# Retention keys and queries and attention keys of the latent rows by seven block products instead of eight, with the context products ahead of them and the modulation sums after them

## The chip, the cores and the metric

The kernel runs on one core of one Trainium2 chip. The metric is the device time of one execution in microseconds (us). TensorE multiplies matrices (operands in SBUF, results in PSUM); VectorE (DVE in the profile), ScalarE (ACT) and GpSimd (POOL) work elementwise; SyncE (SP) mostly issues DMAs. Each engine executes its own queue in order; semaphores order the engines among each other. The order within each queue is fixed when the kernel is built: a scheduler goes through the instructions by their order in the source, and takes a later one earlier when it is ready before the others.

## What is computed

One layer of a diffusion backbone: 1024 latent tokens and 256 context tokens, width 1024, float32. The part that matters here is the input projection, whose seven column blocks of 512 are retention queries (block 0), retention keys (1), retention values (2), gate (3), attention queries (4), attention keys (5) and attention values (6).

```python
m_lat = sc @ w_mod[l] + b_mod[l]
sh1, sc1, g1, sh2, sc2, g2 = ...
h_lat = rms_norm(x, norm1_g[l]) * (1.0 + sc1) + sh1
h_ctx = rms_norm(ctx, norm1_g[l]) * (1.0 + csc1) + csh1
(rq_l, rk_l, rv_l, rg_l), (dq_l, dk_l, dv_l) = split_heads(h_lat @ w_in, rope_r, rope_d)
(rq_c, rk_c, rv_c, rg_c), (dq_c, dk_c, dv_c) = split_heads(h_ctx @ w_in, None, None)
...
x = x + g1 * y_lat                                  # after retention, attention, output projection
h2 = rms_norm(x, norm2_g[l]) * (1.0 + sc2) + sh2    # then the gated MLP with a conv of width 3
x = x + g2 * conv_ffn(h2, ...)
```

Latent queries and keys are rotated by position (`apply_rope`), context keys are not. Of the context only keys and values are used.

## The kernel before

Every float32 operand of the large products is split into a high and a low half, and `passes` (L128) makes a product of three matmuls: high by high, high by low, low by high. A matmul takes 128 rows of the sum over the width (one k) and up to 512 columns; a full product over the width has 8 k, hence 24 matmuls.

- `hT[a][i]` (L174) are the normalized latent rows, transposed: a = 0 the high half, 1 the low half; i the half of the tokens; 8 k by 512 tokens each. `cT[a]` are the 256 context rows in the same form.
- Weights come in slices of two k: `slice_load` (L186) fetches 512 KB into a raw tile (`raw`, pool `wr`, 2 buffers) and `split_slice` (L195) makes `whi` on ScalarE and `wlo` on VectorE (pool `wp`, 5 buffers of each). `stream_block` issues the four slices of a block. From block 5 on the lists `raw_pools` and `slice_pools` add one more raw buffer and one more pair from the pool `m2p`; after block 0 they drop out again.
- `natural` computes 128 tokens by 512 columns (24 matmuls of 512 columns per tile), `transposed` computes one head (128 columns) by 512 tokens, also 24 matmuls. After each k both call `tick()`, which advances a generator that runs beside: it issues a bit of other work in between.
- `rotated` turns a result of `transposed` by position: ScalarE copies swapped 32- or 64-row parts out of PSUM, VectorE makes two products with the tables (`rtab`) and a sum. Attention keys are then split in two halves (`split_store`) and stored to HBM; retention keys and queries are stored as they are. For retention keys `natural_copy` turns the tile back on TensorE and scales it twice; for retention queries `decayed` multiplies it on GpSimd by `qd`, once for each direction.
- `modulations` computes the four late parts of the modulation (groups 0 to 3: g1, sh2, sc2, g2): 32 weight tiles of 512 KB, each multiplied into a sum by a VectorE operation of 128x1024 (L511), then a few matmuls with ones per group (`modulated2`). It runs beside blocks 5, 1 and 0, one step per 7 ticks.

The order of the stages: block 2 for latents, with the normalization; block 2 for the context; block 5 for latents, in its middle the context keys (`pc`, 256 columns); block 6 for the context; the small terms of decay and lambda (`lg`, `dec`, `qd`, `kd`, `cd`); block 1 for the context and for latents; block 0; then block 3 with the backward states of retention beside it, block 6 with the retention outputs beside it, block 4, attention, output projection (`po`), and the MLP. The MLP's first half already makes its products in the seven-product form (`chain`, `second`, `third`, `fifth` from L1300 on).

## Time and profile before

| what | value |
|---|---|
| time of three runs | 1386.96, 1388.20, 1388.31 us; median 1388.2 |
| span of the profiled execution | 1386.3 us (first to last instruction) |
| TensorE clock granted, mean | 0.999 |
| block 2, context (start to start) | 81.4 to 92.3 us |
| block 5 with context keys | 92.3 to 149.4 us |
| block 6 and block 1, context | 149.4 to 172.7 us |
| block 1, latents | 172.7 to about 221 us |
| block 0, latents | about 221 to 269.4 us |
| block 3, latents | 269.4 to 321.6 us |
| attention ends, output projection begins | about 645 us |
| output projection ends | about 744 us |

The page's lists name lines of the kernel; a line of a helper (L131 to L133 in `passes`) collects many uses, so the tile names beside it tell them apart: `pl` is `transposed`, `pn` is `natural`, `pc` the context keys, `chain`, `second`, `third`, `fifth` the MLP's products, `po` the output projection. The time of a run is a little over its span, since the span leaves out what lies before the first and after the last instruction.

### The profile page before, as it was taken

Reading aid. Unit: us, or ns where it says so; the run is one execution under the profiler, and the core shown is the slowest. Engines: PE = TensorE matmul, PEld = TensorE weight load, DVE = VectorE, ACT = ScalarE, POOL = GpSimd, SP = SyncE. Lnnn points to the kernel's source line nnn. Section 1 sums busy time; section 2 is a strip of 40 time slices with the busy share of each in tenths; the row PEclk is TensorE's granted clock in tenths of the full one; section 3 lists DMA queues with packets and bytes.
Section 4 is the critical chain, followed back from the end, with each engine's and each line's share of the span. In section 5 each row is a group of like instructions: output and inputs, shape, how many; then the busy total and the mean of one; then the engine's idle time right before and its main releaser. Section 6 shows DMA issues by size and latency. Waiting matters only on the chain.

```text
span 1386.3 us, 19666 instructions
## 1 busy us (share of the span) xinstructions
PE 1365.4 (98%) x7028; PEld 1145.9 (83%) x7028; DVE 1018.0 (73%) x1512; ACT 738.6 (53%) x1410; POOL 346.4 (25%) x384
## 2 busy tenths in 40 slices
PE   8999999999999999999999999999999999999997
PEld 6788788888888799998888888888888888888886
DVE  5967866623467898896347998887778877898756
ACT  5536534313466789987037654555545555455533
POOL 1310001501446433411101343222332220043003
PEclk9999999999999999999999999999999999999999
DMA  9467887786678488631221223332323326953334
GB/s 384 153 206 252 295 265 249 254 273 185 191 221 231 133 217 186 140 94 70 106 99 46 92 107 114 114 114 92 114 100 113 111 69 224 393 180 109 122 99 152
DMA packets 107305, 231.14 MB, mean 167 GB/s; under 512 B 9604, under 2 KB 42884, under 8 KB 105288
## 3 DMA queue, kind: packets, MB, share of 16 engines
q1 hardware_dynamic: 98936, 204.73, 43.3%
q0 software_dynamic: 8128, 24.91, 7.9%
q8 instruction: 55, 0.90, 0.3%
q14 instruction: 42, 0.34, 0.1%
q10 hardware_dynamic: 144, 0.26, 0.1%
HBM read 165.37 MB, written 64.23 MB: 166 GB/s over the span
## 4 chain that ended last, share of the span: by engine, by line
PE 65%; DVE 1%; POOL 1%; issue 0%; ACT 0%; DMA 0%; SPq 0%; POOLq 0%; ACTq 0%; DVEq 0%
PE chain L131 6%; PE chain L132 6%; PE chain L133 6%; PE c L132 5%; PE c L133 5%; PE c L131 5%; PE pv L929 5%; PE pA L897 5%; PE third L131 3%; PE third L133 3%; PE third L132 3%; PE pt L917 2%; PE po L133 2%; PE po L132 2%; PE po L131 2%; PE second L131 1%
## 5 line engine op out<-in xcount | busy, mean ns | idle before, releaser
L131 PE MATMUL pl<-hT,whi 128*128 128x512 f32 x256 | 107.6, 420 | 0.0
L131 PE MATMUL chain<-T,whi 128*128 128x512 f32 x264 | 102.8, 389 | 0.0
L132 PE MATMUL chain<-T,whi 128*128 128x512 f32 x264 | 102.7, 389 | 0.0
L133 PE MATMUL chain<-T,wlo 128*128 128x512 f32 x264 | 102.7, 389 | 0.0
L133 PE MATMUL pl<-hT,wlo 128*128 128x512 f32 x256 | 100.4, 392 | 0.0
L132 PE MATMUL pl<-hT,whi 128*128 128x512 f32 x256 | 100.3, 392 | 0.0
L900 DVE TENSOR_REDUCE mt<-pA 128x1 f32<-128x1280 f32 x64 | 95.2, 1490 | 3.8 <-PE pA L897 2.3
L133 PE MATMUL c<-whi,ghl 128*128 128x512 f32 x232 | 90.4, 390 | 0.0
L131 PE MATMUL c<-whi,ghl 128*128 128x512 f32 x232 | 90.3, 389 | 0.0
L132 PE MATMUL c<-wlo,ghl 128*128 128x512 f32 x232 | 90.3, 389 | 0.0
L1310 POOL TENSOR_TENSOR cmb<-wrb 128x512 f32<-128x512 f32 x20 | 30.3, 1517 | 237.6 <-DMA wrb<-w_up 157.3
L897 PE MATMUL pA<-ks,qhl 128*128 128x512 f32 (+1 forms) x384 | 89.6, 368 | 0.0
L904 ACT ACTIVATE p<-pA,mt 128x1280 f32<-128x1280 f32 x64 | 85.5, 1336 | 3.8 <-DVE mt L900 3.4
L131 PE MATMUL pn<-whi,hT 128*128 128x512 f32 x192 | 85.0, 443 | 0.0
L445 ACT ACTIVATE xb<-pl 32x512 f32<-32x512 f32 (+1 forms) x88 | 52.0, 591 | 61.6 <-PE pl L133 41.9
L1161 ACT CAST whi<-cmb 128x512 fp32r<-128x512 f32 x62 | 38.4, 622 | 77.5 <-PE chain L132 64.3
L929 PE MATMUL pv<-va,aT 128*128 128x128 f32 x640 | 77.1, 276 | 0.4 <-DVE yT L958 0.3
L897 PEld LDWEIGHTS pA<-ks,qhl 128*128 128x128 f32 x384 | 67.9, 189 | 11.5
L133 PE MATMUL pn<-whi,hT 128*128 128x512 f32 x192 | 75.8, 396 | 1.0 <-POOL hT L610 1.0
L132 PE MATMUL pn<-wlo,hT 128*128 128x512 f32 x192 | 75.4, 393 | 0.0
L929 PEld LDWEIGHTS pv<-va,aT 128*128 128x128 f32 x640 | 74.0, 192 | 1.2 <-DVE yT L958 0.8
L1162 DVE TENSOR_TENSOR wlo<-cmb,whi 128x512 fp32r<-128x512 f32 x62 | 58.7, 951 | 18.1 <-ACT whi L1161 18.1
(336 smaller groups left out, 3889.7 us busy)
## 6 DMA issues: line engine op xcount, KB each, us to landing
raw<-w_in SPq DMA_DIRECT2D x32, 512.0 KB, 6.0
wm<-w_mod SPq DMA_DIRECT2D x32, 512.0 KB, 4.6
wra<-w_up SPq DMA_DIRECT2D x24, 512.0 KB, 3.3
wrb<-w_up SPq DMA_DIRECT2D x23, 512.0 KB, 3.5
W<-w_down SPq DMA_DIRECT2D x44, 256.0 KB, 6.2
ad<-s SPq DMA_DIRECT2D x20, 512.0 KB, 3.4
wra<-ad SPq DMA_DIRECT2D x20, 512.0 KB, 3.3
wrb<-ad SPq DMA_DIRECT2D x18, 512.0 KB, 4.6
```

Source lines behind the costliest of these rows:

```text
L131: mm(ps, lh, rh, start=first, stop=False, skip_group_check=more)
L132: mm(ps, lh, rl, start=False, stop=False, skip_group_check=more)
L133: mm(ps, ll, rh, start=False, stop=last, skip_group_check=more)
L445: nc.scalar.activation(xb[q * blk : (q + 1) * blk, :], pt[o : o + blk, :], AF.Copy, scale=scale)
L897: mm(self.pa[m][:, c0:c1], self.q[:, i, m, qs], self.k[:, m, c0:c1], start=(i == 0), stop=(i == 1))
L900: nc.vector.tensor_reduce(out=self.mt[:, m : m + 1], in_=self.pa[m][:, :LK], axis=AX.X, op=ALU.min)
L904: nc.scalar.activation(self.p[m], self.pa[m][:, :LK], AF.Exp, scale=-1.0, bias=self.mt[:, m : m + 1], accum_out=self.s[:, m : m + 1])
L917: nc.tensor.transpose(self.pt[g][:, i, :], self.p[0][:, (4 * g + i) * P : (4 * g + i + 1) * P], ident)
L929: mm(self.pv, self.aT[:, c, :], self.v[:, c, :], start=(c == 0), stop=(c == NKT - 1))
L1161: nc.scalar.copy(hi, src)
L1162: nc.vector.tensor_tensor(out=lo, in0=src, in1=r32(hi), op=ALU.subtract)
L1310: nc.gpsimd.tensor_tensor(out=s1, in0=b1, in1=b2, op=ALU.add)
```

## The change

For blocks 5, 1 and 0 the latent rows (1024 wide, 1024 tokens) and the weights of two heads (1024 by 256) are cut in two by two blocks, and the four result blocks (two heads by two halves of tokens) are made from seven block products of half the width (4 k each) in place of eight. The sums and differences of weights (`combined`) are made on GpSimd, those of the rows (T1 to T4) on GpSimd and VectorE while the context products run. T1 takes the place of the first half of `hT[a][1]`, which is put aside in HBM (`h12_d`) and fetched back for block 3; T4 takes the place of `cT` once the context is done with. So the context products of blocks 2, 6, 1 and 5 come first, one after the other. Modulation groups 0 and 3 now run beside blocks 3 and 6, groups 1 and 2 beside the output projection. The weights come from a second copy in HBM (`w_pair`), two heads' worth per pair. The extra raw and slice buffers of `m2p` are gone. The swap of rotated parts becomes DMAs from SBUF to SBUF, except for one of the four results.

```diff
+PAIRED = (5, 1, 0)
...
-        raw_pools = [lambda: wr] * 2
-        slice_pools = [lambda: wp] * 5
...
+        for a in range(2):
+            nc.sync.dma_start(out=h12_d[a], in_=r32(hT[a][1][:, 0:4, :]))
...
+        B11, B21 = (tuple(hT[a][0][:, c : c + 4, :] for a in range(2)) for c in (0, 4))
+        T1, B22 = (tuple(hT[a][1][:, c : c + 4, :] for a in range(2)) for c in (0, 4))
+        T2, T3 = (tuple(tq.tile([P, 4, 512], F32R, name=f"tq{i}{a}") for a in range(2)) for i in (2, 3))
+        T4 = tuple(head_rows(t.rearrange("p k l -> p (k l)")) for t in cT)
...
+        def split_to(src, tt, c):
+            nc.scalar.copy(tt[0][:, c, :], src)
+            nc.vector.tensor_tensor(out=tt[1][:, c, :], in0=src, in1=r32(tt[0][:, c, :]), op=ALU.subtract)
+
+        def whole(name, hf, k, bufs=2):
+            o = tm.tile([P, 512], F32, name=name, bufs=bufs)
+            nc.gpsimd.tensor_tensor(out=o, in0=r32(hT[0][hf][:, k, :]), in1=r32(hT[1][hf][:, k, :]), op=ALU.add)
+            return o
...
+        def fourth_sums():
+            for c, t2 in enumerate(second):
+                t4 = whole("r12", 0, c + 4)
+                nc.gpsimd.tensor_tensor(out=t4, in0=t4, in1=t2, op=ALU.subtract)
+                split_to(t4, T4, c)
+
+        beside(block_sums(), 0.24, 0.0)
+        natural(wget, ctx_lhs, range(NTC), store_to(kvg_row(ROW_V), center=True))
+        wg = stream_block(6)
+        natural(wg, ctx_lhs, range(NTC), store_to(dv_row))
         wg = stream_block(1)
-        rtab = load_rope(0)
+        small_terms()
         natural(wg, ctx_lhs, range(NTC), context_decayed)
-        transposed(wg, [q[:, :, 1] for q in rqk_d], rtab, 64, RET_SCALE, 0, by_head, True)
-        wg = stream_block(0)
-        transposed(wg, [q[:, :, 0] for q in rqk_d], rtab, 64, 1.0, 0, by_head, also=decayed)
+        wg = stream_block(5)
...
+        beside(iter(()), 0.0)
+        fourth_sums()
...
+        er = erS.enter_context(tc.tile_pool(name="er", bufs=2, reuse_waits="tile"))
...
+        first_ops = [er.tile([P, 2, 4, P], F32R, name="xhl") for _ in range(2)]
...
+                self.ops = dict(p1=a1, p2=a2, p3=b1, p4=b2, p5=s1, p6=s2, p7=s3)
+                self.combos = ((s1, b1, b2, ALU.add), (s2, s1, a1, ALU.subtract), (s3, a1, b1, ALU.subtract), (b1, a2, s2, ALU.subtract))
...
+            def product(self, ps, p, tt, first):
+                o = self.halves.pop(p)
+                for k in range(4):
+                    passes(ps, (o[:, 0, k, :], o[:, 1, k, :]), (tt[0][:, k, :], tt[1][:, k, :]), first and k == 0, k == 3, not first)
+                    tick()
...
+            def turned(self, u, xb, c, hf):
+                cs, sn = self.rtab(hf)
+                (nc.vector if self.block == 0 else nc.gpsimd).tensor_tensor(out=xb, in0=xb, in1=sn, op=ALU.mult)
+                nc.vector.tensor_tensor(out=u, in0=u, in1=cs, op=ALU.mult)
+                nc.vector.tensor_tensor(out=u, in0=u, in1=xb, op=ALU.add)
+                self.kept(u, c, hf)
...
+            def begin(self):
+                self.chain = ps_a.tile([P, 512], F32, name="chain", tag="mm")
+                self.product(self.chain, "p1", B11, True)
+                second = ps_b.tile([P, 512], F32, name="second", tag="mm")
+                self.product(second, "p2", B21, True)
+                u = self.copied()
+                self.plus(u, second)
+                self.u11 = u, self.swapped(u)
...
+            def seventh(self):
+                self.product(self.chain, "p7", T3, False)
+                u = self.copied()
+                self.plus(u, self.other)
+                self.u22 = u, self.swapped(u)
+
+            def third(self):
+                self.product(self.other, "p3", B22, False)
+                self.plus(self.u12, self.other)
+                self.u12 = self.u12, self.swapped(self.u12)
...
+        for j in range(N_PAIRS):
+            one, more = prs[j], j + 1 < N_PAIRS
...
+            one.sixth()
...
+            one.fifth()
+            one.turned(*one.u11, 0, 0)
...
+            one.seventh()
...
+            if j > 0:
+                prs[j + 1].begin()
+            one.turned(*one.u22, 1, 1)
...
+            one.third()
...
+            one.fourth()
...
+        also(modulations((0, 3), ..., 6, ...), 1.0, 0.0)
...
+        beside(modulations((1, 2), norm_weights, norm_sums, 4, lambda: pst, None), 1.0)
```

The pairs go in the order two of block 5, then one of block 1, one of block 0, one of block 1, one of block 0. `begin` of pairs 0 and 1 comes ahead of the loop; from pair 2 on it stands between `seventh` and `third` of the pair before. `block_sums` makes T1, T2 and T3 chunk by chunk like `fourth_sums`. The last pair's `third` and `fourth` are issued inside the first tile of block 3.

More of the change, by code (lines that the diff above doesn't have):

```diff
@@ L405, in natural @@
                     tick()
+                    if inside and k == 3:
+                        inside()
+                        inside = None
                 finish(t, pt)
@@ new lines @@
+        beside(iter(()), 0.0)
+        fourth_sums()
+        tmS.close()
+        smallS.close()
+        erS = ExitStack()
+        er = erS.enter_context(tc.tile_pool(name="er", bufs=2, reuse_waits="tile"))
+        rp = erS.enter_context(tc.tile_pool(name="rp", bufs=3, reuse_waits="tile"))
+        hi_tag, lo_tag = dict(tag="whi", bufs=5), dict(tag="wlo", bufs=5)
+        sums = [wp.tile([P, 2, 4, P], F32, name="cmb", **t) for t in (hi_tag, lo_tag)]
+        sums = itertools.cycle([t[:, i] for t in sums for i in range(2)])
@@ new lines, in last_end @@
+        def last_end():
+            one.turned(*one.u22, 1, 1)
+            one.split("p4")
+            one.third()
+            one.fourth()
+            one.turned(*one.u12, 0, 1)
+            for _ in range(4):
+                turn_one()
+        wg = stream_block(3)
+        for a in range(2):
+            nc.gpsimd.dma_start(out=hT[a][1][:, 0:4, :], in_=h12_d[a])
+        natural(wg, lat_lhs, range(1), store_to(kvg_row(ROW_G), func=AF.Silu, c0=NTC), last_end)
+        erS.close()
+        qdS.close()
@@ L1819, in lay_out @@
         "w_in": kmajor(a["w_in"][0], 7),
+        "w_pair": kmajor(np.concatenate([a["w_in"][0][:, 512 * b : 512 * (b + 1)] for b in PAIRED], axis=1), 4 * len(PAIRED)),
         "w_out": kmajor(a["w_out"][0], 2),
```

391 lines of the change are left out of this document (261 added, 130 removed).

## The prediction

> **What bounds the kernel now.** I read the page's head first: span, busy shares and clock.
>
> ```profile
> span 1386.3 us, 19666 instructions
> ...
> PE 1365.4 (98%) x7028; PEld 1145.9 (83%) x7028; DVE 1018.0 (73%) x1512; ACT 738.6 (53%) x1410; POOL 346.4 (25%) x384
> ...
> PEclk9999999999999999999999999999999999999999
> ```
>
> TensorE works for 1365.4 of 1386.3 us at full clock, so only 21 us of the span are TensorE waiting. The list of its waits (in all, times, longest) names none above 1.3 us:
>
> ```profile
> PE pyt L311 <- POOL y L307: 1.3, 1, 1.3
> ...
> PE third L131 <- DVE ub L1433: 0.7, 1, 0.7
> ...
> PE pn L132 <- DVE wlo L197: 0.5, 2, 0.3
> ```
>
> The span is a stream of matmuls, and it shortens only if matmuls go away. Next I cut the part that the change touches into its stages with the view by stretches (columns: length, busy time of PE, PEld, DVE, ACT, POOL, clock, DMA share, GB/s): context products of blocks 6 and 1, latent keys (block 1), latent queries (block 0), then block 3.
>
> ```profile
> 148.00:161.00 13.00, 12.67 (x55) 10.08 (x55) 12.63 (x16) 8.39 (x12) 0.00 (x0) 1.00 0.93 328
> 161.00:173.00 12.00, 11.81 (x51) 9.12 (x50) 7.59 (x8) 2.60 (x3) 0.00 (x0) 1.00 0.95 321
> 173.00:221.00 48.00, 48.00 (x232) 39.91 (x231) 29.15 (x37) 19.90 (x30) 0.96 (x1) 1.00 0.79 254
> 221.00:269.40 48.40, 48.40 (x221) 39.39 (x220) 31.32 (x38) 17.30 (x26) 23.84 (x14) 1.00 0.79 255
> 269.40:321.60 52.20, 52.20 (x264) 43.92 (x263) 18.42 (x42) 9.81 (x13) 2.55 (x2) 1.00 0.81 261
> ```
>
> In both latent blocks TensorE has no idle time. VectorE is busy for about 60%, GpSimd for 2% and 49%.
>
> **The gain.** A group's mean duration is no price, because neighbouring matmuls overlap. The price is the distance between starts, from the timeline of TensorE: the first and the 24th product of block 1.
>
> ```profile
> 172.69 0.39 PE L131 MATMUL pl<-hT,whi 128*128 128x512 f32 x1
> ...
> 177.90 0.39 PE L133 MATMUL pl<-hT,wlo 128*128 128x512 f32 x1
> ```
>
> (177.90 − 172.69) / 23 = 0.2265 us. Blocks 5, 1 and 0 now take 3 blocks × 8 (head, half) × 8 k × 3 passes = 576 such matmuls. The new scheme has six pairs of heads, each with 7 products × 4 k × 3 passes: 504. The 72 that go are worth 72 × 0.2265 = **16.3 us**. Context products, transposes of keys and modulation matmuls keep their number and only move.
>
> **What it adds on the path.** First, weight slices. The old code had three raw buffers and six pairs of split buffers from block 5 on; the new one has two and five, and now three context products of 10.9 us (48 matmuls) follow each other. The old kernel shows one change of block with exactly two and five, block 3 to 6.
>
> ```profile
> 317.76 1.23 DVE L197 TENSOR_TENSOR wlo<-raw,whi 128x1024 fp32r<-128x1024 f32 x1 [0.51 <-ACT whi L196]
> 319.02 2.26 SPq L189 DMA_DIRECT2D raw<-w_in  x2
> 323.15 1.05 ACT L196 CAST whi<-raw 128x1024 fp32r<-128x1024 f32 x1 [0.77 <-DMA raw<-w_in]
> 324.23 1.23 DVE L197 TENSOR_TENSOR wlo<-raw,whi 128x1024 fp32r<-128x1024 f32 x1 [1.93 <-ACT whi L196]
> ...
> 315.01 0.48 PE L131 MATMUL pn<-whi,hT 128*128 128x512 f32 x1
> ...
> 321.67 0.48 PE L131 MATMUL pn<-whi,hT 128*128 128x512 f32 x1
> ...
> 325.89 0.39 PE L131 MATMUL pn<-whi,hT 128*128 128x512 f32 x1
> ```
>
> The second slice's low half frees a raw buffer (319.02), the fourth slice lands 4.1 us later and is split by 325.46; k = 6 asks for it at 325.89. That margin of 0.4 us exists because state matmuls stretch each k to 0.83 us before the border ((321.67 − 315.01) / 8); without them (3 × 0.2265 = 0.68) the chain begins some 0.8 us later. Estimate: 0.3 us late at 2→6 and at 6→1. The context keys of block 5 are 256 wide.
>
> ```profile
> 119.94 0.28 PE L132 MATMUL pc<-cT,whi 128*128 128x256 f32 x1
> 120.06 0.28 PE L133 MATMUL pc<-cT,wlo 128*128 128x256 f32 x1
> ```
>
> At 0.12 us apiece, head 0 reaches k = 6 after 18 × 0.12 = 2.2 us instead of 4.1, so it waits about 2 us. Sum 2.6; bounds 0 (earlier loads) and 7 (three slices behind a busy VectorE).
>
> Second, the start of the pairs, which I take as the largest loss. `fourth_sums` writes over the context rows (`T4` is `cT`), so its casts begin only as the last context head passes k = 1, about 2 us before the end of that stage. Its temporaries `r12` have two buffers: chunks 2 and 3 must wait for the splits of 0 and 1, and each costs two GpSimd operations. By my count of bytes the first operand tiles (`first_ops`, from the pool `er`) lie where `r12` lay, so the cast of p1 follows the last split. Durations:
>
> ```profile
> L430 POOL TENSOR_TENSOR xq<-xa,qd x16: 1282/1296/2283, 232.8 to 274.3; 128x512 f32<-128x512 f32 x16
> ...
> L1161 ACT CAST whi<-cmb 128x512 fp32r<-128x512 f32 x62 | 38.4, 622 | 77.5 <-PE chain L132 64.3
> ...
> L1162 DVE TENSOR_TENSOR wlo<-cmb,whi x62: 673/691/1779, 776.3 to 1146.6; 128x512 fp32r<-128x512 f32 x62
> ```
>
> The first split is over 0.7 us before the stage ends (2.0 − 0.62 − 0.69). From there: 4 × 1.30 + 0.62 + 0.69 + 0.62 = 7.1, less 0.7: **6.4 us** in which TensorE has nothing else to do. Bounds: 0 if the tiles don't overlap, 9 if `cT` comes free only whole. The raw weights of pair 1 land meanwhile.
>
> Third, in pair 0 `third` follows `seventh` directly and writes the bank that `plus` still reads: a copy and a sum of the FFN's kind.
>
> ```profile
> L1296 ACT COPY ua<-chain 128x512 f32<-128x512 f32 x11 | 6.4, 582 | 0.0
> ...
> L1422 DVE TENSOR_TENSOR ua<-third,ua 128x512 f32<-128x512 f32 x11 | 7.6, 692 | 10.6 <-PE third L133 10.6
> ```
>
> 0.58 + 0.69, with some 0.3 for drain and signals (estimate): **1.6 us**, once; from pair 1 on, `begin` of the next pair (24 matmuls, 5.4 us) stands between.
>
> Fourth, the pairs themselves. The FFN already runs seven products in this way:
>
> ```profile
> 780.00:820.00 40.00, 40.00 (x178) 33.14 (x177) 39.65 (x41) 23.67 (x35) 23.11 (x12) 1.00 0.33 118
> 820.00:860.00 40.00, 39.25 (x174) 32.18 (x173) 36.93 (x40) 20.35 (x30) 16.22 (x9) 1.00 0.32 119
> 900.00:940.00 40.00, 40.00 (x178) 33.10 (x177) 30.93 (x36) 20.10 (x29) 12.33 (x10) 1.00 0.28 99
> ```
>
> Even with VectorE busy for 39.65 of 40 us TensorE did not stop; once it lost 0.75. The new pairs have 23 (block 5), 19 (block 1) and 22 (block 0) VectorE operations of 128x512 in 84 × 0.2265 = 19.0 us; 128 in all at 0.69 are 88 of 114 us. I take 1.2 us of stalls; bounds 0 and the slower rival below. ScalarE has 7 × 0.62 plus four to ten copies, 11 to 13 us of 19: cover enough. The swaps of halves become 48 DMAs of SP; what queues behind them there are stores, for which nothing waits soon, and the raw weights of the pair after next, about one pair (19 us) ahead of their use.
>
> Fifth, what moves. Modulations 0 and 3 go to blocks 3 and 6, 1 and 2 to the output projection: 16 steps each.
>
> ```profile
> L511 DVE SCALAR_TENSOR_TENSOR macc<-wm,csil,macc 128x1024 f32<-128x1024 f32 x30 | 38.4, 1280 | 7.9 <-DMA wm<-w_mod 7.7
> ...
> 674.93 0.69 DVE L1242 TENSOR_TENSOR gated<-po,g 128x512 f32<-128x512 f32 x1 [2.89 <-PE po L133]
> 675.65 0.69 DVE L1243 TENSOR_TENSOR x<-gated,x 128x512 f32<-128x512 f32 x1
> 680.37 0.69 DVE L1242 TENSOR_TENSOR gated<-po,g 128x512 f32<-128x512 f32 x1 [4.02 <-PE po L133]
> ```
>
> In the projection VectorE idles 4.0 of each 5.4 us; two steps of 1.28 fit. A step that waits for its weights holds up state updates or the emptying of `po` behind it on VectorE; the 30 steps shown waited 7.7 us in all and TensorE never for them. In blocks 3 and 6 their 8 MB meet a DMA share already at 0.81, together with 2 MB of rows of `hT` fetched back through GpSimd's queue. I take 0.3 us; bounds 0 and 6.
>
> **Sum.** 2.6 + 6.4 + 1.6 + 1.2 + 0.3 = 12.1 against 16.3: **4.2 us less**. The profiled span becomes 1386.3 − 4.2 = 1382.1. The runs shown took 1386.96 to 1388.31, up to 2.0 us more than the span; that edge stays, so from the median 1388.2 I predict **1384.0 us**.
>
> **Rivals.** (a) *The covers hold*: the pool's layout or an earlier order hides the start, slices arrive in time, and only pair 0 and about 4 us of small waits remain: 16.3 − 5.3 = 11.0, 1377. For it: in the whole old span TensorE loses 0.5 us to slices. Against it: the chain behind `cT` has no other cover.
>
> (b) *Slower: VectorE and GpSimd exclude each other in the pairs.* The 691 ns median and 1779 ns maximum of L1162 differ by most of one GpSimd operation, so one can stop the other. If all of them alternate, 104 VectorE operations on SBUF alone at 0.60 (their distance when queued, estimate from the 0.69 rows) and 52 GpSimd operations (24 sums, 12 sine products, 16 decays) at 1.30 need 62 + 68 = 130 us, while TensorE with its key transposes needs 118. That is 12 more, in place of the 1.2 for the pairs and with pair 0's 1.6 inside it: 1384.0 − 1.2 − 1.6 + 12 = 1393. It decides from 123 us on, that is unless at least five of the last decays may run on under block 3. The Trainium skill, "SBUF — State Buffer", section "SBUF: two separate sides", calls this port pair an exclusive lock held for a whole instruction; the maximum agrees. Against (b): the FFN row with 39.65 and 23.11 us busy cost TensorE nothing.
>
> (c) *The clock falls after the gap at the start.* If TensorE comes back at half speed for the 12 matmuls of p1, 12 × 0.2265 = 2.7 us are added: 1386.7. No row shows it, as its longest wait is 1.3 us. The Trainium skill, "TensorE: Matmul & The Clock Gate", Part 1 (the HAM clock gate), has the clock halved after an idle window of about 3.4 us and restored after as long a busy one; no run here shows that.
>
> (d) *The moved modulations stall block 3, 6 or the projection*: 16 steps late by 0.3 us are 5: 1389.
>
> **How the numbers follow.** Forecast 0.38 (its own range 1381 to 1387), (a) 0.26, (b) 0.22, (c) 0.07, (d) 0.07. Some 0.2% (2.8 us) is about what a measurement of this kernel can tell from no change: faster means below 1385.4. Of the forecast's 0.38 I put 0.26 there and 0.12 within; with (a) that is 0.52 faster; 0.12 + (c) + most of (d) is 0.24 within; (b) and the rest 0.24 slower. The range runs from inside (a) to (b): 1374 to 1394.
>
> **What would show it.** TensorE idle of 5 to 8 us between the last `pc` and the first `chain`, released by ScalarE's or VectorE's split; about 2 us in `pc` on VectorE's low half; 1.6 us before the first `third`; 504 matmuls at 0.227; no wait on `macc` in the projection. I am wrong if the start gap is under 3 us (then (a)), or if waits of `chain` and `third` for splits sum to over 6 us with VectorE and GpSimd both near full (then (b)).

## The result, and the profile after

The changed kernel is slower: 1473.78 us (median of four runs, 1471.24 to 1478.95) against 1388.26 us (1386.96 to 1389.01), a ratio of 1.062 with a 95% interval of 1.0598 to 1.0643. The forecast was 1384.0, its range ended at 1394.

The page's head of the changed kernel (span, busy shares, granted clock):

```profile
span 1473.7 us, 19904 instructions
...
PE 1378.3 (94%) x6956; PEld 1149.2 (78%) x6956; DVE 1108.1 (75%) x1579; ACT 751.3 (51%) x1436; POOL 441.6 (30%) x446
...
PEclk9988798998999999999999999999999999999999
```

The 72 matmuls are gone (7028 to 6956), yet TensorE is busy 12.9 us longer, and it idles 95.4 us where it idled 20.9. The clock row, all nines before, has eights and a seven in its first quarter. I summed TensorE's busy time times (1 − granted clock) over stretches of 2 us from 60 to 860 us: 0.0 before, 24.6 us now. So the span's 87.4 us are 74.5 of idle time, some 24.6 of half-speed work and 4.6 that I do not assign, minus the 16.3 forecast as gain.

TensorE's waits (in all, times, longest), where the old list had none above 1.3 us in this part:

```profile
PE chain L184 <- ACT xhl L939: 14.1, 1, 14.1
PE pn L184 <- ACT whi L245: 10.5, 3, 7.4
PE pub L402 <- DMA kvgb<-kvg: 9.5, 1, 9.5
PE pk L530 <- DVE xa L968: 7.5, 3, 5.7
PE pn L185 <- DVE wlo L246: 5.0, 2, 3.9
PE pk L530 <- DVE xa L512: 4.2, 2, 3.3
...
PE chain L186 <- DVE xhl L940: 3.1, 1, 3.1
...
PE fifth L184 <- DVE xa L955: 2.2, 1, 2.2
```

They lie in four places, and the view by stretches (columns as in the prediction) shows them stage by stage: context products, the gap ahead of the first `chain`, the pairs, blocks 3 and 6. Below it are two rows of the kernel before, for the whole section until block 3 and for blocks 3 and 6.

```profile
82.60:151.30 68.70, 51.48 (x241) 41.47 (x239) 54.77 (x78) 27.95 (x53) 29.86 (x20) 0.85 0.52 167
151.30:165.60 14.30, 0.26 (x3) 0.06 (x1) 10.56 (x9) 4.83 (x10) 14.22 (x10) 0.60 0.18 61
165.60:312.00 146.40, 126.31 (x513) 100.21 (x513) 104.02 (x117) 55.46 (x93) 65.16 (x43) 0.90 0.55 173
312.00:469.60 157.60, 138.64 (x708) 116.53 (x706) 79.14 (x176) 49.80 (x137) 38.33 (x54) 0.94 0.80 268
```

```profile
81.40:269.40 188.00, 187.48 (x889) 154.60 (x888) 128.29 (x187) 85.90 (x146) 25.76 (x16) 1.00 0.79 259
269.40:390.30 120.90, 120.90 (x673) 104.28 (x672) 50.14 (x141) 40.50 (x115) 26.94 (x45) 1.00 0.71 222
```

From the first context product to block 3 it is 229.4 us instead of 188.0, and blocks 3 and 6 take 157.6 instead of 120.9, of which 5.4 are the last pair's 24 products and 3.4 the eight `pg` matmuls of modulation groups 0 and 3, which only moved there. Attention and projection together take 284.8 instead of 276.3.

The first stretch says why. These are the timelines of VectorE and of GpSimd while T1 to T3 are made beside the context products:

```profile
89.41 1.77 DVE L836 TENSOR_TENSOR hT<-r,hT 128x512 fp32r<-128x512 f32 x1
91.11 1.78 DVE L836 TENSOR_TENSOR tq<-r,tq 128x512 fp32r<-128x512 f32 x1
92.81 1.78 DVE L836 TENSOR_TENSOR tq<-t,tq 128x512 fp32r<-128x512 f32 x1
94.51 0.67 DVE L475 TENSOR_REDUCE mu<-st 128x4 f32<-128x512 f32 x1
...
96.20 1.22 DVE L476 TENSOR_SCALAR mu<-mu 128x4 f32<-128x4 f32 x1
97.33 0.68 DVE L853 TENSOR_TENSOR r<-t,r 128x512 f32<-128x512 f32 x1
```

```profile
87.66 1.28 POOL L840 TENSOR_TENSOR t<-hT,hT 128x512 f32<-128x512 f32 x1
88.90 1.74 POOL L856 TENSOR_TENSOR t<-t,r 128x512 f32<-128x512 f32 x1
90.60 3.44 POOL L840 TENSOR_TENSOR t<-hT,hT 128x512 f32<-128x512 f32 x2
94.00 3.39 POOL L840 TENSOR_TENSOR r<-hT,hT 128x512 f32<-128x512 f32 x2
```

The same kind of VectorE operation takes 0.68 us at 97.33 and 1.78 at 91.11; a correction of 128x4 takes 1.22. GpSimd takes 1.28 us when VectorE is out of the way and about 1.7 otherwise. While both have work, their starts are 1.70 us apart, one each in turn (89.41, 91.11, 92.81). That is the look of a lock. The Trainium skill, "SBUF — State Buffer", section "SBUF: two separate sides", says that a VectorE operation with two inputs in SBUF and a GpSimd operation that reads SBUF exclude each other for a whole instruction and that `tensor_reduce` never contends on trn2; the 1.78 us and the undisturbed 0.67 us of the reduction agree.

But other readings fit the waits too. The theories that went into the runs were: **lock** (VectorE stands still while GpSimd works, and everything that needs a split comes late), **order** (casts of row sums stand ahead of slice casts on ScalarE, raw loads behind blocked stores on SyncE, key transposes ahead of products on TensorE), **moved modulation** and **late inputs** for blocks 3 and 6, and the **half clock** after idle time (TensorE granted half of its clock).

### The profile page after: what moved, and what is told of

It is laid out like the page before. It is cut to its first block, busy times and chain, and to the rows that moved or that the text cites. A ratio compares the mean times of both kernels' runs of the same rounds, so it can differ in the third digit from the quotient of the medians.

```text
span 1473.7 us, 19904 instructions
## 1 busy us (share of the span) xinstructions
PE 1378.3 (94%) x6956; PEld 1149.2 (78%) x6956; DVE 1108.1 (75%) x1579; ACT 751.3 (51%) x1436; POOL 441.6 (30%) x446
## 4 chain that ended last, share of the span: by engine, by line
PE 58%; DVE 3%; issue 1%; ACT 1%; DMA 1%; POOL 1%; SPq 0%; POOLq 0%; DVEq 0%; ACTq 0%
PE chain L184 5%; PE chain L185 5%; PE chain L186 5%; PE c L185 5%; PE c L184 5%; PE c L186 5%; PE pA L1144 4%; PE pv L1176 4%; PE third L184 2%; PE third L186 2%; PE third L185 2%; PE po L184 2%; PE po L186 2%; PE po L185 2%; PE pt L1164 2%; PE second L184 1%
## 5 line engine op out<-in xcount | busy, mean ns | idle before, releaser
L185 PE MATMUL c<-wlo,ghl 128*128 128x512 f32 x232 | 90.3, 389 | 0.0
L184 PE MATMUL c<-whi,ghl 128*128 128x512 f32 x232 | 90.3, 389 | 0.0
L1408 ACT CAST whi<-wra 128x512 fp32r<-128x512 f32 x55 | 33.8, 622 | 90.9 <-PE third L185 43.5
L184 PE MATMUL third<-yT,whi 128*128 128x512 f32 x168 | 65.5, 390 | 1.6 <-DVE ub L1687 1.6
L186 PE MATMUL third<-yT,wlo 128*128 128x512 f32 x168 | 65.5, 390 | 0.0
L185 PE MATMUL third<-yT,whi 128*128 128x512 f32 x168 | 65.4, 389 | 0.0
```

The source lines that it names most:

```text
L184: mm(ps, lh, rh, start=first, stop=False, skip_group_check=more)
L185: mm(ps, lh, rl, start=False, stop=False, skip_group_check=more)
L186: mm(ps, ll, rh, start=False, stop=last, skip_group_check=more)
L1408: nc.scalar.copy(hi, src)
```

## The experiments

Stages of each run in us, from the starts of TensorE's matmuls in its trace. "Until 3" is from the first context product to the first product of block 3; "att." runs from the last `pl` to the first product of the projection, "proj." to the first product of the MLP. Block 6 is counted from the start of block 3's last product, and block 3 of every changed kernel holds the last pair's 24 products (5.4 us). The time is one run (medians for the first two rows); runs of the kernel before on the same chips took 1387.05 to 1388.68.

| kernel | time | context | gap | pairs | until 3 | block 3 | block 6 | att. | proj. |
|---|---|---|---|---|---|---|---|---|---|
| before | 1388.3 | | | | 188.0 | 52.2 | 68.7 | 177.6 | 98.7 |
| changed | 1473.8 | 68.7 | 14.4 | 146.3 | 229.4 | 67.4 | 90.3 | 181.8 | 103.0 |
| e1_sums_vector | 1448.8 | 53.9 | 10.7 | 141.6 | 206.2 | 64.9 | 88.3 | 183.5 | 103.8 |
| e2_pairs_vector | 1433.4 | 68.2 | 8.7 | 116.6 | 193.6 | 61.9 | 84.9 | 181.9 | 105.8 |
| e3_both_vector | 1412.8 | 53.9 | 7.0 | 117.8 | 178.7 | 62.5 | 81.4 | 181.9 | 103.1 |
| e4_no_late_mod | 1457.7 | 70.3 | 13.6 | 143.1 | 227.0 | 70.7 | 70.6 | 183.5 | 102.6 |
| e5_no_mod_steps | 1398.6 | 53.9 | 5.9 | 117.8 | 177.5 | 62.3 | 70.6 | 183.5 | 98.7 |
| e6_warm_gap | 1420.6 | 52.6 | 9.1 | 115.0 | 176.6 | 64.1 | 84.8 | 183.5 | 103.2 |
| e7_states_later | 1415.3 | 55.1 | 5.9 | 116.7 | 177.7 | 61.7 | 84.5 | 183.5 | 102.9 |
| e8_first_ops | 1410.3 | 54.2 | 1.8 | 115.3 | 171.3 | 63.8 | 82.0 | 182.0 | 103.6 |
| e9_shadow | 1455.4 | 65.8 | 12.8 | 135.7 | 214.3 | 65.1 | 83.9 | 183.4 | 103.5 |
| e10_steps_only | 1407.5 | 54.6 | 6.6 | 118.7 | 179.8 | 61.9 | 75.5 | 182.2 | 103.2 |
| e11_loads_only | 1412.6 | 55.2 | 6.7 | 118.7 | 180.5 | 61.7 | 83.6 | 177.5 | 105.1 |
| e12_halves_queue | 1407.7 | 53.7 | 1.2 | 119.3 | 174.3 | 69.2 | 76.7 | 179.0 | 102.6 |
| e13_no_row_sums | 1406.7 | 49.1 | 0.1 | 118.6 | 167.7 | 62.4 | 83.3 | 183.4 | 103.6 |

### Lock or order: who does the sums

**e1_sums_vector**, the row sums on VectorE:

```diff
-            nc.gpsimd.tensor_tensor(out=o, in0=r32(hT[0][hf][:, k, :]), in1=r32(hT[1][hf][:, k, :]), op=ALU.add)
+            nc.vector.tensor_tensor(out=o, in0=r32(hT[0][hf][:, k, :]), in1=r32(hT[1][hf][:, k, :]), op=ALU.add)
...
-                nc.gpsimd.tensor_tensor(out=t2, in0=t2, in1=t1, op=ALU.subtract)
+                nc.vector.tensor_tensor(out=t2, in0=t2, in1=t1, op=ALU.subtract)
...
-                nc.gpsimd.tensor_tensor(out=t4, in0=t4, in1=t2, op=ALU.subtract)
+                nc.vector.tensor_tensor(out=t4, in0=t4, in1=t2, op=ALU.subtract)
```

> The 24 GpSimd operations that make the row sums (T1 to T4, first sums and three kinds of differences) go to VectorE; all else as in the changed kernel (1473.8 us). Theory 'lock': while GpSimd works, every VectorE operation takes 1.75 us instead of 0.68 and so the splits of weight slices come late. Then the context products fall from 69.3 us to 46 to 52, the gap ahead of the first chain from 13.7 to 7 to 10 (pair sums stay on GpSimd there), and the time to about 1440 to 1455. Theory 'order': the stage is long because casts that wait for row sums stand ahead of the slices' casts on ScalarE, and raw loads behind blocked stores on SyncE; who makes the sums matters little: context products 64 to 70 us, time within 5 us of 1473.8.

**e2_pairs_vector**, the pairs' GpSimd work on VectorE (`combined`, the sine product in `turned`, `decayed`):

```diff
-                    nc.gpsimd.tensor_tensor(out=o, in0=a, in1=b, op=op)
+                    nc.vector.tensor_tensor(out=o, in0=a, in1=b, op=op)
...
-                (nc.vector if self.block == 0 else nc.gpsimd).tensor_tensor(out=xb, in0=xb, in1=sn, op=ALU.mult)
+                nc.vector.tensor_tensor(out=xb, in0=xb, in1=sn, op=ALU.mult)
```

> The 24 weight sums, the 12 sine products and the 16 decay products of the pairs go from GpSimd to VectorE; the row sums stay on GpSimd. 'Lock': the context products stay at 69 us; the gap falls from 13.7 to 9 to 11 us, since weight sums no longer alternate with the row sums; VectorE then holds about 104 + 52 operations at 0.6 to 0.69 (94 to 108 us) plus copies beside 113 us of products, so the pairs fall from 146 us to 122 to 132: time about 1445 to 1460. 'Order': key transposes in TensorE's queue and swaps by DMA set the pairs' length; they stay within 4 us of 146, or grow as VectorE is nearly full: time 1470 to 1480.

**e3_both_vector** has both edits.

> Both moves together: no elementwise work on GpSimd from the context products to the end of the pairs. 'Lock': gains of the two add: context products 46 to 52 us, gap 6 to 8, pairs 122 to 132, time 1410 to 1430; blocks 3 and 6 keep their 37 us of loss, so it stays above 1388. 'Order': within 8 us of 1473.8.

Stretches of e3 (context products and pairs):

```profile
82.20:136.10 53.90, 48.83 (x240) 40.86 (x239) 45.57 (x95) 28.66 (x52) 0.00 (x0) 0.94 0.63 205
...
143.10:260.90 117.80, 116.64 (x508) 93.94 (x509) 101.50 (x163) 55.60 (x94) 1.34 (x2) 0.97 0.65 204
```

VectorE does 17 more operations in the context stage (78 to 95) and is busy 9 us less (54.77 to 45.57). In the pairs it does 46 more and is busy no longer (104.02 to 101.50), and the pairs shrink by 28.5 us. Of these, 19 us were idle time of TensorE (146.40 less 126.31, against 117.80 less 116.64) and 10 its work at the lower clock (126.31 against 116.64). Each edit takes effect mainly in its own stage, and together they give 61.0 us. e2's pairs came out 5 us better than the range the lock theory gave, e1's context stage 2 us worse than its own. The order theory expected no change, and ScalarE, whose queue it blames, does the same work as before (53 and 52 operations in the context stage, 93 and 94 in the pairs). It was right about where the pairs' waits appear: the list above has 11.7 us of waits at key transposes (`pk`) for turned keys (`xa`), out of 20.1 us of idle time. But these waits go when GpSimd's work goes, with the order in the source left as it was.

Another reading remains: a sum on VectorE need not be handed from one engine to another. **e9_shadow** keeps the sums on VectorE and gives GpSimd additions whose results nobody reads:

```diff
+        def again(a, pool, w, n):
+            for _ in range(n):
+                scr = pool.tile([P, w], F32, name="scr", bufs=1)
+                nc.gpsimd.tensor_tensor(out=scr, in0=a[:, :w], in1=r32(hT[0][0][:, 0, :w]), op=ALU.add)
...
                 split_to(t1, T1, c)
+                again(r32(T1[1][:, c, :]), tm, 512, 2)
...
                     nc.vector.tensor_tensor(out=o[:, 1], in0=self.ops[p], in1=r32(o[:, 0]), op=ALU.subtract)
+                    again(r32(o[:, 1].rearrange("p a b -> p (a b)")), er, 192, 2)
```

> Base: all sums on VectorE (1412.8 us). GpSimd is given work that nobody reads: after each split of a row sum one or two additions of 128x512 (24 in all), after each split of a pair two of 128x192 (84 in all), each from a finished half tile into a scratch tile. No engine waits for them but the release of the temporaries ahead of the first operands. Theory 'lock' (VectorE stands still while GpSimd works): context products grow from 53.9 us to 62 to 72, VectorE's 128x512 operations beside them take up to 1.7 us, the pairs grow from 117.8 to 130 to 150, time 1440 to 1465. Theory 'hand-over' (the moves to VectorE gained only because a result no longer passes between engines): context products and pairs stay within 2 us of the base, time 1411 to 1416.

VectorE and GpSimd in e9 at 88 to 92 us, and the stretch of its pairs:

```profile
87.96 1.78 DVE L477 TENSOR_TENSOR st<-st,mu 128x512 f32<-128x512 f32 x1
89.67 0.68 DVE L845 TENSOR_TENSOR r<-hT,hT 128x512 f32<-128x512 f32 x1
...
91.48 1.78 DVE L845 TENSOR_TENSOR t<-hT,hT 128x512 f32<-128x512 f32 x1
```

```profile
87.50 1.70 POOL L841 TENSOR_TENSOR scr<-tq,hT 128x512 f32<-128x512 f32 x1
91.10 1.61 POOL L841 TENSOR_TENSOR scr<-tq,hT 128x512 f32<-128x512 f32 x1 [1.90 <-DVE tq L836]
```

```profile
160.70:296.40 135.70, 120.56 (x508) 95.30 (x509) 123.50 (x161) 54.47 (x92) 82.30 (x86) 0.95 0.57 178
```

VectorE's 1.78 us fall where a GpSimd addition runs, and its 0.68 where none does. The useless work costs 11.9 us in the context stage, 17.9 in the pairs and 42.6 us in all. So the lock costs time where nothing is handed over. It brings back 11.9 of the 14.8 us of the context stage but, with GpSimd busy for 82.30 us instead of 65.16, only 17.9 of the 28.5 of the pairs. The rest may be that in the changed kernel results on the way to TensorE pass through GpSimd; no run separates that. (Part of the gap's growth is the scratch tile, which lies in the memory that the first operands wait for.)

### What the start costs, and the clock

**e8_first_ops** (on e3) splits pair 0's first operands before T4, into slice buffers that are already free:

```diff
+        early_ops = [wp.tile([P, 2, 4, P], F32R, name="pop", **t) for t in (hi_tag, lo_tag)]
+        for p, c, o in (("p1", 0, early_ops[0]), ("p2", 4, early_ops[1])):
+            nc.scalar.copy(o[:, 0], raw_tiles[0][0][:, c : c + 4, :])
+            nc.vector.tensor_tensor(out=o[:, 1], in0=raw_tiles[0][0][:, c : c + 4, :], in1=r32(o[:, 0]), op=ALU.subtract)
+            first_halves[p] = o
         fourth_sums()
...
-        first_ops = [er.tile([P, 2, 4, P], F32R, name="xhl") for _ in range(2)]
```

> Base: all sums on VectorE (1412.8 us). The first operands p1 and p2 of pair 0 lie in free slice buffers instead of the memory of the row sums' temporaries, and are split ahead of T4. Theory 'start gap' (my recorded third step: only the place of the first operands makes TensorE wait for T4): the wait of 6.7 us ahead of the first chain falls under 1.5 us and the clock stays 1.0 there, so block 3 begins 7 to 9 us earlier: time 1404 to 1406. Rival: the next wait takes its place, for pair 1's raw weights or for p6 and p5 behind T4's splits on VectorE: block 3 begins only 2 to 4 us earlier.

The wait of 6.7 us is gone from TensorE's list and the section until block 3 is 7.4 us shorter, so the place of those two tiles was the cause. The run as a whole gained 2.5: its context stage began 1.7 us later than in e3, and blocks 3 and 6 took 1.9 us more.

**e6_warm_gap** (on e3) fills the gap with eight small matmuls after each split of T4:

```diff
                 split_to(t4, T4, c)
+                dm = pst.tile([P, 4, P], F32, name="dm", tag="tr")
+                for i in range(8):
+                    mm(dm[:, i % 4, :], ones, r32(T4[0][:, c, :P]), start=True, stop=True)
```

> Base: all sums on VectorE (1412.8 us), where TensorE waits 6.7 us ahead of the first chain and its 12 matmuls then lie 0.427 us apart at a granted clock of 0.50. After each of the four splits of T4 eight small matmuls (ones by 128 columns of T4, into a tile that nobody reads) keep TensorE busy. Theory 'idle halves the clock': the chain's matmuls lie 0.227 apart and the start of `second` comes 2 to 2.6 us earlier after the first chain matmul; the wait itself stays. Theory 'the low clock belongs to the stage' (power or DMA load): spacing stays 0.43.

The first chain's matmuls in e3 and in e6:

```profile
143.08 0.79 PE L184 MATMUL chain<-hT,xhl 128*128 128x512 f32 x1 [6.68 <-ACT xhl L939]
...
144.83 0.63 PE L184 MATMUL chain<-hT,xhl 128*128 128x512 f32 x1
145.25 0.63 PE L185 MATMUL chain<-hT,xhl 128*128 128x512 f32 x1
```

```profile
144.94 0.40 PE L184 MATMUL chain<-hT,xhl 128*128 128x512 f32 x1
145.18 0.39 PE L185 MATMUL chain<-hT,xhl 128*128 128x512 f32 x1
```

Starts are 0.42 to 0.43 us apart in e3 and 0.23 in e6 (0.24 in these two rows): the idle time, not the stage, halves the clock. From the first chain matmul to `second` it is 2.85 us instead of 5.59. The run itself came out 7.8 us longer than e3. The chain began later (the gap is 9.1 us instead of 7.0), and block 3 waited for its slices (1.8, 0.8 and 3.2 us at 269 to 278 us), which e3 does not; why block 6 took 3.4 us more is not traced. So this is a test and no remedy.

### Blocks 3 and 6

**e4_no_late_mod** (on the changed kernel) and **e5_no_mod_steps** (on e3, all four groups, `if groups:`) leave the modulation steps out:

```diff
+        if 0 in groups:
+            for n, i in enumerate(groups):
+                acc = sum_tile(n)
+                nc.gpsimd.memset(acc, 0.0)
+                nc.sync.dma_start(out=acc[0:1, :], in_=rows[:, R_BMOD + (2 + i) * D : R_BMOD + (3 + i) * D])
+                yield
+                yield from modulated2(i, acc, pool, rows_out)
+            return
```

> The modulation groups 0 and 3 leave out their 16 weight tiles and VectorE steps: g1 and g2 are their bias rows alone; the matmuls with ones, the stores and all else stay. Blocks 3 and 6 took 52.2 and 68.7 us before and take 67.8 and 89.8 in the changed kernel. Theory 'modulation' (16 steps of 1.28 us on VectorE and 8 MB of loads stall the states and outputs): they return to within 4 us of 52 and 69, time about 1440. Theory 'late inputs' (decay tables, states' loads and stores of the pairs come late, whatever the modulation does): block 3 keeps 8 us or more of its loss, block 6 half of it; time 1455 or more.

> Base: the kernel with all sums on VectorE (1412.8 us). All four modulation groups leave out their weight tiles and VectorE steps (g1, sh2, sc2, g2 are then their bias rows alone). The run without groups 0 and 3 showed block 6 at 70.6 instead of 90.3 us, block 3 unchanged. Theory 'moved modulation': block 6 falls from 81.4 to 69 to 71, attention and projection from 285.0 to 276 to 278 (before: 276.3), block 3 stays at 58 to 62: time 1390 to 1394. Theory 'elsewhere' (attention's tail and block 6 are late for other reasons, the state of PSUM or stores of the pairs): attention and projection stay above 282, time above 1398.

Without the steps block 6 takes 70.6 us in both runs, 19.7 (on the changed kernel) or 10.8 (on e3) less. Not all of that is gain. The eight `pg` matmuls of groups 0 and 3 (0.43 us apart, 3.4 us) run in block 6 in the changed kernel and in e3, but in block 3 in these two runs, where they wait for the bias rows in `macc` (6.8 us in e4, 1.7 in e5). So block 3 does not shorten (70.7 after 67.4, 62.3 after 62.5), and what the steps cost is better read from both blocks together: 16.4 us on the changed kernel, 11.0 on e3. Of e4's two theories, modulation was right for block 6, late inputs for block 3 and for the time (1457.7). In e5 the projection returns to 98.7, but attention does not shorten: near its end it now holds the 32 small matmuls of groups 1 and 2 (4.7 us at 643.6). The time of 1398.6 missed the expected 1390 to 1394.

**e10_steps_only** and **e11_loads_only** cut the modulation in two (on e3):

```diff
-            if n + 2 < len(steps):
-                step_load(n + 2)
-            nc.vector.scalar_tensor_tensor(out=acc, in0=wms.pop(n), scalar=csil[:, k, 0:1], in1=acc, op0=ALU.mult, op1=ALU.add)
+            nc.vector.scalar_tensor_tensor(out=acc, in0=wms[n % 2], scalar=csil[:, k, 0:1], in1=acc, op0=ALU.mult, op1=ALU.add)
```

> Base: all sums on VectorE (1412.8 us); without any modulation step block 6 fell from 81.4 to 70.6 us and the projection from 103.1 to 98.7. Here all 32 VectorE steps of 1.28 us stay, but the weight tiles of steps 2 and on are left out: every step multiplies one of the first two. Theory 'VectorE' (the 1.28 us steps stand ahead of states, scores and outputs in its queue): block 6 stays at 79 to 83, projection at 102 to 104. Theory 'DMA' (8 MB of loads beside the kvg and qk tiles): block 6 falls to 70 to 73, projection to 99 to 100.

```diff
-            nc.vector.scalar_tensor_tensor(out=acc, in0=wms.pop(n), scalar=csil[:, k, 0:1], in1=acc, op0=ALU.mult, op1=ALU.add)
+            nc.vector.scalar_tensor_tensor(out=acc[:, 0:16], in0=wms.pop(n)[:, 0:16], scalar=csil[:, k, 0:1], in1=acc[:, 0:16], op0=ALU.mult, op1=ALU.add)
```

> The other half of the run before: all 32 weight tiles are loaded, but each step multiplies 16 of 1024 columns. Theory 'VectorE': block 6 falls to 70 to 73 us, projection to 99 to 100, time 1397 to 1401. Theory 'DMA': block 6 stays at 79 to 83 (waits of puc and pub for kvg tiles stay), time 1410 or more. If both runs lie halfway, the two costs add.

Block 6 in e3, in e10 and in e11:

```profile
323.40:404.80 81.40, 76.80 (x440) 64.02 (x439) 44.02 (x115) 31.59 (x107) 25.06 (x45) 1.00 0.81 270
```

```profile
324.00:399.60 75.60, 75.46 (x441) 64.31 (x439) 39.17 (x114) 32.69 (x107) 24.68 (x44) 1.00 0.71 232
```

```profile
324.40:408.10 83.70, 77.24 (x441) 64.01 (x439) 35.23 (x115) 31.90 (x107) 24.12 (x45) 1.00 0.81 264
```

I had expected VectorE to be the price. The loads alone keep block 6 at its full length (83.7 us with a DMA share of 0.81), and TensorE is idle in it for 6.5 us (83.70 less 77.24). With the steps alone it is idle for 0.1 us (75.60 less 75.46). The 5.0 us by which e10's block 6 is longer than e5's are mostly work that e5 does in block 3, the `pg` matmuls (3.4 us) and eight small ones of the states (1.1). So in block 6 the loads are the price. In attention it is the other way round: with short steps it takes 177.5 us, as before the change, with full ones 182, though the projection is then 2.0 us longer. The remaining 4.4 us of the projection are no loss at all. They are the 32 small matmuls of groups 1 and 2 (4.5 us in both profiles), which before lay beside blocks 1 and 0.

Block 3's loss has its own cause. SyncE's queue of the changed kernel as block 3 runs (start, length, DMA), GpSimd beside it, and the wait that follows on TensorE:

```profile
337.41 0.36 SPq L492 DMA_DIRECT2D rqk<-xq  x1
...
338.49 0.68 SPq L1085 DMA_DIRECT2D dec<-consts  x1
...
340.31 1.68 SPq L283 DMA_DIRECT2D kvgb<-kvg  x3
```

```profile
334.86 2.53 POOL L491 TENSOR_TENSOR xq<-xa,qd 128x512 f32<-128x512 f32 x2 [2.49 <-DVE xa L968]
```

```profile
346.49 1.19 PE L402 MATMUL pub<-kvgb 128*128 128x128 f32 x4 [9.52 <-DMA kvgb<-kvg]
```

The store of the last decay holds the queue until 337.41. Only then can the decay tables and the first `kvgb` be asked for, and TensorE starts on `kvgb` 6.2 us after its issue. The row of `macc` that e4 waits for stands in the same queue.

**e7_states_later** (on e3: `beside(states, 36 / 48, -10.0)`) was to let the states wait for them.

> Base: all sums on VectorE (1412.8 us). The backward states beside block 3 begin 7.5 ticks (about 5.5 us) later and run at 36/48 per tick instead of 36/58, so they end at the same place. In the base TensorE waits 5.3 us for the first kvgb, asked for only when the last decays have left SyncE's queue. Theory 'late inputs': that wait goes, the clock there stays at 1.0, and block 3 falls from 62.5 to 55 to 58 us: time 1405 to 1408. Theory 'density': the states' chain on VectorE among modulation steps sets the pace, and the wait returns later as one for puc, pub or PSUM: within 2 us of 1412.8.

It did not do so: the first `pub` stands at the same place in TensorE's order as in e3, since the scheduler takes it ahead as soon as it thinks it ready, and the wait stays (5.7 us). This run does not decide between its theories.

**e12_halves_queue** (on e8) halves the modulation steps and fetches `kvgb` through GpSimd's queue:

```diff
+                    c = slice(0, 512) if t == 0 else slice(512, D)
+                    nc.vector.scalar_tensor_tensor(out=acc[:, c], in0=wms[n][:, c], scalar=csil[:, k, 0:1], in1=acc[:, c], op0=ALU.mult, op1=ALU.add)
...
+            (nc.gpsimd if nm == "b" else nc.sync).dma_start(out=kvg[:, :n], in_=kvg_d[g][:, h, r0 : r0 + n])
```

> The kernel with the first operands in free slice buffers (1410.3 us), with two edits more: each modulation step is two of 512 columns, half a step's ticks apart, and the kvgb tiles of the backward states are fetched through GpSimd's DMA queue in place of SyncE's. Theory 'queues' (block 3 waits since kvgb stands behind stores and dec, mk, gn on SyncE; block 6 since 1.28 us steps hold VectorE): the wait of 5.4 us for the first kvgb falls under 2 us, block 6 from 82.0 to 75 to 79: time 1399 to 1404. Rival: the tiles' memory comes free only with the last decays, and 32 us of VectorE are 32 us in any cut: within 3 us of 1410.

Its longest group of waits takes the place of the old one. Below it are SyncE's queue, ScalarE and VectorE ahead of the longest of them, which ends at 295.8:

```profile
PE pub L404 <- DVE Sb L298: 6.0, 4, 3.4
```

```profile
282.64 0.36 SPq L494 DMA_DIRECT2D rqk<-xq  x1
...
283.72 0.81 SPq L1091 DMA_DIRECT2D dec<-consts  x1
```

```profile
291.17 1.28 ACT L1101 ACT_TABLE_LOAD   x1 [11.61 <-DMA dec<-consts]
```

```profile
292.90 0.88 DVE L1102 TENSOR_TENSOR dec<-dec,mk 128x128 f32<-128x128 f32 x3 [5.70 <-ACT dec L1101]
...
295.36 0.79 DVE L298 SCALAR_TENSOR_TENSOR Sb<-Sb,cd,pub 128x128 f32<-128x128 f32 x2
```

The wait for the `kvgb` DMA went, block 6 fell to 76.7, and block 3 grew from 63.8 to 69.2. The other input behind the last decay's store now holds it: the decay tables (`dec`) still stand in SyncE's queue, ScalarE gets them at 291.2, VectorE sits idle for 5.7 us until they come to it, and the state step `Sb` stands behind them. So the theory named the right queue, and the run took only one of two inputs out of it. The sum of the two blocks is unchanged (145.9 against 145.8). The time is 2.6 us better than e8's and still 19 us behind the kernel before. No version here beats that kernel.

### What was left in the context stage

**e13_no_row_sums** (on e3) splits T1 to T4 from rows as they are:

```diff
-                r12 = whole("r12", 1, c)
-                t1 = whole("r11", 0, c)
-                nc.vector.tensor_tensor(out=t1, in0=r12, in1=t1, op=ALU.subtract)
-                split_to(t1, T1, c)
+                for tt in (T1, T3, T2):
+                    split_to(r32(hT[0][0][:, c, :]), tt, c)
```

> Base: all sums on VectorE (1412.8 us), context products 53.9 us where 16 row-sum operations and 12 splits of T1 to T3 stand among the slices' splits on VectorE (before: 45.6 us without them). The 24 row sums are left out: T1 to T4 are split from rows of the first half as they are, so the keys and queries are not the reference's. Theory 'VectorE is full' (busy 10 of 10 us from 80 to 120): context products fall to 46 to 49 us and no slice is late by more than 0.5 us. Theory 'slices' (my recorded first step: two raw and five pairs of buffers, narrow context keys): they stay at 51 to 54, with the same 2.2 us wait of the context keys. The wait ahead of the first chain falls as well, since no temporaries hold the first operands' memory; that is not what this run asks.

```profile
82.20:131.20 49.00, 45.84 (x240) 38.34 (x239) 32.10 (x72) 25.59 (x50) 0.00 (x0) 1.00 0.72 232
```

The stage falls to 49.1 us (expected 46 to 49), and its six waits for slice halves sum to 3.2 us, the longest 0.8. The four context stages of the kernel before took 45.6 us. So of e3's 8.3 us more, 4.8 go with the row sums on VectorE (with the half clock after its one wait of 2.2 us), and the 3.5 that e13 keeps are about those six waits.

## Why the prediction was wrong

**The gain** of 16.3 us stood on a good price. At full clock the products lie 0.23 us apart, as forecast, and 72 are gone.

**The step that failed** is the fourth of what the change adds: "I take 1.2 us of stalls" for the pairs, on the ground that the MLP ran with VectorE busy for 39.65 and GpSimd for 23.11 of 40 us and TensorE did not stop. Moving GpSimd's work off shortened the pairs by 28.5 us, 19 of them waits of TensorE and 10 work at the lower clock. The row of the MLP proved less than I read in it. The 62 operations of L1162 in its group have a mean of 951 ns beside the median of 691, so busy time there holds the time in which an operation stands before the lock. And TensorE ran only products in that stretch, while in the pairs its own key transposes wait for turned keys that come out of the two engines (11.7 us in five waits). That the MLP also needs its results later is my reading and not tested.

**Rival (b)** named this mechanism, with a chance of 0.22 and 12 us, and missed its size twice. It looked only at the pairs, while the same lock works where the row sums are made; for VectorE's splits of slices in that stage I had no term but bounds of 0 and 7. Taking GpSimd out gave 14.8 us there, 7.4 in the gap, 28.5 in the pairs and 13.8 in blocks 3 and 6, where the first wait for `kvgb` falls from 9.5 to 5.3: 64.5, of which 61.0 reach the time. And it weighed the sum of both queues, 130 us, against TensorE's 118. Where the two alternate, one operation of each takes 1.70 us, so the 52 of GpSimd and the 104 of VectorE would need about 120 (an estimate, 52 × 1.70 + 52 × 0.60). That is below the 123 from which I let the rival decide, and the stage took 146.3. What costs is not the sum of the queues but each late result that TensorE waits for. I had quoted the tell-tale, the 1779 ns maximum beside a median of 691, and asked only whether one engine's total filled the stage.

**Slices** (2.6 us): the mechanism was right where nothing else disturbs them, and the sum nearly, 3.2 us in e13. The parts were not: 1.2 and 0.7 us at the two changes of block, where I had 0.3 each, and 1.3 at the context keys instead of 2. So the sum owes something to luck. **The start** (6.4): right in cause, as e8 shows, and 6.7 us in e3; in the changed kernel, where the two engines alternate, 14.1 and then 3.1 more. **`third` of pair 0** (1.6): 2.2 us (`fifth` in the list of waits, the bank that it writes), but 1.8 in e13 and nothing in e3. In the changed kernel `plus` stood behind a turned result that waited 1.2 us for GpSimd, so the likeness of 1.6 and 2.2 is partly luck, and no run shows the 0.3 that I put in for drain and signals.

**The clock**, rival (c), was priced as one gap of 2.7 us. That price was right for that gap (e3 against e6: 2.74). But nine stretches between 99 and 469 us ran at half clock, and all of it comes to 24.6 us.

**Moved modulation** (0.3, bounds 0 and 6): sized wrongly. Leaving it out saves 14.2 us on e3, and groups 0 and 3 alone 16.0 on the changed kernel. The projection, where I looked for room on VectorE, was free but for its own small matmuls; attention's end, where the steps in fact begin, pays 4.4. Block 6 pays most, by loads at a DMA share of 0.81 (TensorE idle for 6.5 us with the loads alone, 0.1 with the steps alone), a share that I quoted for block 3 and set aside. **Late inputs of block 3** had no term at all; the decay tables and the first `kvgb` wait for the last decay's store. That this queue is the cause is read from the traces, of e12 above all, where the wait passes from `kvgb` to the tables; no run took both out of it, so what that would gain is not shown.

What I read off the old profile, that the span is a stream of matmuls and shortens only if matmuls go away, held while TensorE had no waits in this section. The change removed the slack that made it true.

## What to carry to other kernels

Before moving elementwise work to an idle engine, count where VectorE and GpSimd would both read SBUF at the same time: there they take turns, and a busy share does not show it, since it includes the standing still. Then ask which single result TensorE waits for, since both queues can have room in all and that result still come late. Price a new wait on TensorE twice, once for its length and once for the half-speed matmuls after it. A stage's length after an edit says little until one has looked whether work moved across its border (the `pg` matmuls here). And work that "only moves" needs a look at what it meets at its new place: which loads, which chain of small steps, and whose queue it stands in.

## What the runs showed that I had not expected

Two queues under the lock take turns one for one: starts of VectorE and GpSimd are 1.70 us apart, so a VectorE that would do an operation in 0.60 does one in 1.70. A small operation stands too: one of 128x4 took 1.22 us instead of 0.15.

The clock goes by windows and not by single waits. In the clock records of the 15 traces, from 60 to 860 us, each of the 130 stretches of full or half clock lasts a whole number of 3.413 us. These are two waits of 3.3 us (`pc`, near 130 us) laid out on that grid, in e6 and then in e1 (columns as before; e1's clock of 0.51 is 0.50 with a rounded edge):

```profile
127.21:130.63 3.42, 1.75 (x15) 1.55 (x13) 0.00 (x0) 3.42 (x15) 0.00 (x0) 1.00 0.82 299
130.63:134.04 3.41, 1.81 (x15) 1.84 (x16) 2.83 (x5) 1.38 (x5) 0.00 (x0) 1.00 0.46 139
134.04:137.45 3.41, 3.41 (x32) 3.41 (x32) 3.33 (x7) 2.54 (x6) 0.00 (x0) 1.00 0.61 178
```

```profile
130.49:133.90 3.41, 1.40 (x12) 1.43 (x13) 1.89 (x3) 1.38 (x6) 0.44 (x1) 1.00 0.37 120
133.90:137.32 3.42, 2.90 (x15) 2.60 (x13) 3.13 (x4) 2.15 (x5) 3.42 (x3) 0.51 0.53 159
```

In e6 the wait is shared by two windows, TensorE is busy for half of each, and the clock stays. In e1 most of it lies in one window, busy for 1.40 us, and the next window runs at half. In all 15 traces each of the 62 windows at full clock in which TensorE was busy for less than 0.43 of the time was followed by half clock, and of the 3285 that were busy for at least half only five were. Full clock came back only after windows busy for 0.82 or more. So a wait of 1.8 us can cost the clock (e6, `pn` at 269.4, with 0.8 more behind it) and one of 3.3 us need not; each one of 3.7 us or more that began at full clock in this section did. The Trainium skill, "TensorE: Matmul & The Clock Gate", Part 1 (the HAM clock gate), has a window of 3413 ns that runs free of the program, and the traces agree. The rule that the prediction took from there, half clock after an idle window, is narrower than what they show: a window busy for up to 0.43 was enough, and the measurement decides.
